# The first unit of an up-projection as eight plain products, with its rows first in the last attention head

## The chip, the cores and the metric

The kernel runs on one core of a Trainium2 chip. The core has a matrix engine (TensorE, called PE; PEld is its loading of weights), a vector engine (VectorE, DVE), an engine for activations and copies (ScalarE, ACT), a general engine (GpSimd, POOL), and a queue that only issues transfers here (SyncE, SP). Each engine works off its own queue in order. Matmul results go to eight PSUM banks; all else lies in SBUF, in buffers that are handed out from pools. The metric is the time of one execution on the device in microseconds (us), as the median of several runs.

## What is computed

One inference step of a one-layer encoder. Rows are 1024 new prompt frames with 16 learned meta rows ahead of them, and 32 frames of a running stream, 1072 rows in all, 1024 wide. Four mixers run side by side (RG-LRU, forgetting attention, stick-breaking attention, gated DeltaNet). Their concatenated, normalised outputs go through `w_o`, are added to the residual and layer-normalised; then comes a convolutional feed-forward part with D_FF = 2816:

```python
x = layer_norm(ALPHA * x + m, P['ln1_g'][l], P['ln1_b'][l])     # m: the mixers through w_o
f, fbuf = conv_ffn(x, st_l['ffn_conv'], P['ffn_w_in'][l], P['ffn_conv_w'][l], P['ffn_conv_b'][l], P['ffn_w_out'][l])
x = layer_norm(ALPHA * x + f, P['ln2_g'][l], P['ln2_b'][l])

def conv_ffn(x, buf, w_in, conv_w, conv_b, w_out):
    gate, up = jnp.split(x @ w_in, 2, axis=-1)
    gate_c, new_buf = causal_dwconv(gate, buf, conv_w, conv_b)
    return (jax.nn.gelu(gate_c) * up) @ w_out, new_buf
```

Everything is fp32. Each large product is made of three matmuls on a high and a low half of both operands: `hi` is a rounded copy (ACT), `lo` the rest (a subtraction), and hi·hi + lo·hi + hi·lo is summed in PSUM.

## The kernel before, in words

The rows lie in nine blocks: block 0 has 48 rows (32 running frames, 16 meta rows), blocks 1 to 8 have 128 each. The program is written as a sequence with priorities, and a planner makes each engine's queue from it: whenever an engine is free in the planner's own account, it takes the instruction with the lowest priority number among those that are ready. A tile from a pool has to wait for a buffer, also where a new pool is laid over the memory of an old one.

*The end of the attention* (`attention`, L1444). Heads run one after the other, the four stick-breaking ones ("s") and then the four forgetting ones ("f"). Each head visits the row blocks in the order `ROWS`, one block in a step (block 8 takes two). Value products are made for the blocks (7, 8), (0, 1, 2), (5, 6) and (3, 4) together. In the last head a finished block goes on at once: `w_o_units("f")` (L1733) multiplies it by the mixer's part of `w_o`, two halves of six matmuls, and DVE adds the scaled result to `h` (L181); two blocks later `ln1_rows` (L1822) takes its statistics on DVE, normalises it on ACT (L144) and stores it as `hn` (SP, L1832). The order of the blocks there is `WROWS`.

*The up-projection* (`ffn_up`, L2017). D_FF is cut into 22 feature tiles of 128; a unit is a pair of them, for the gate (even units) or for the up half (odd units), so there are 22 units. The rows are cut into two parts: part 0 holds blocks 5 to 8 (512 columns, two halves L and R of 256), part 1 blocks 0 to 4 (two halves of 274, which overlap by two). The 1024 inputs are cut in two halves as well, 1 and 2. So an operand is L1, R1, L2 or R2, and a unit times a part is a 2x2 product by blocks. It is made in seven products in place of eight (Strassen in Winograd's form): with sums of operands T1 = R1 - L1, T2 = R2 - T1, T3 = R2 - R1, T4 = L2 - T2 and with four sums of weights (`w_sums`, L1926). Each product (`ffn_product`, L1954) is 12 matmuls (L1959). `STEPS` gives the seven with their PSUM banks a, b, c; `ffn_evac` (L1962) combines the banks: ft is a copy, `fu` is ft plus bank b, after which bank b is added to again by T3, then fv and the outputs.

*Its beginning* (`x_ops`, L1867). For each part, `x_turn` (L1836) transposes the rows on PE and ACT and DVE take them out with gain and bias as `xr` (left half on ACT, L144; right half on DVE, L178). Then the four sums and the seven splits into `xh` and `xl` are made, the sums on DVE except T1, the splits' low halves on DVE for L1, T2, T3, T4 and on POOL for L2, T1, R2. Unit 0 runs part 0 whole and then part 1 whole, its weights split anew for each; from unit 1 on both parts take each step together. `w_load` (L1913) loads a unit's weights in two transfers, `w_split` (L1937) makes a step's halves (ACT, POOL) into four buffers, some steps ahead. `ffn_conv` (L2002) makes convolution and GeLU of a gate tile when its unit ends: four sums on DVE (L181) for each tile, two activations on ACT and the GeLU.

Of the kernel before, what the change touches and what calls it, by code (L numbers as in the profile page):

```python
# [16 lines left out]
P = 128  # L17
# [35 lines left out]
class Gen:  # L53
# [97 lines left out]
    @contextmanager  # L151
    def first(self):

        p = self.tc.cur_priority
        self.tc.cur_priority = p - 100000
        yield
        self.tc.cur_priority = p + (self.tc.cur_priority - (p - 100000))

# [203 lines left out]
    def split_w(self, src, ap, n, m, after=None, gain=None):  # L362
# [13 lines left out]
        return hi, lo  # L376

# [1066 lines left out]
    def attention(self, past):  # L1444

        runs = [(key, h, j, c) for key in "sf" for h in range(4) for j in ROWS for c in reversed(self.attn_chunks(j))]
# [29 lines left out]
        while t < len(runs) + 5 or pairs or late:  # L1476
# [46 lines left out]
            while late and late[0][0] <= t:  # L1523
# [5 lines left out]
                if i > 1:  # L1529
                    self.ln1_rows(WROWS[i - 2])  # L1530
            t += 1
# [335 lines left out]
    def x_ops(self, part, tags, between):  # L1867

        nc = self.nc
        w = NP[part][2]  # L1870
        tags = iter(tags)
        new = lambda: self.U("xr", F32, 4 * w)
        v = lambda t: t.rearrange("p (k m) -> p k m", k=4)
        ops = self.xo[part] = {}

        def split(name, t, eng):
            hi, lo = (self.U(x, F32R, 4 * w, next(tags)) for x in ("xh", "xl"))
            self.act(hi, t, AF.Copy)
            self.tt(lo, t, hi.bitcast(F32), OP.subtract, eng)
            ops[name] = v(hi), v(lo)  # L1880
            between()

        def turn(half):
            l, r = new(), new()
            for k in range(4):
                self.x_turn(part, 4 * half + k, [v(l)[:, k], v(r)[:, k]])
            return l, r

        l1, r1 = turn(0)
        t1 = new()  # L1890
        self.tt(t1, r1, l1, OP.subtract, nc.gpsimd)
        between()
        split("L1", l1, nc.vector)
        l2, r2 = turn(1)
        t2, t3 = l1, r1
        self.tt(t2, r2, t1, OP.subtract)
        split("T2", t2, nc.vector)
        split("L2", l2, nc.gpsimd)
        self.tt(t3, r2, r1, OP.subtract)
        split("T3", t3, nc.vector)  # L1900
        split("T1", t1, nc.gpsimd)
        self.tt(l2, l2, t2, OP.subtract)
        split("T4", l2, nc.vector)
        split("R2", r2, nc.gpsimd)

    def ln1(self):
# [4 lines left out]
        self.xo = {}  # L1911
# [36 lines left out]
    def ffn_steps(self, u):  # L1948

        if u == 0:  # L1950
            return [(n, i) for n in range(2) for i in range(7)]
# [453 lines left out]
```

## Time and profile before

| what | value |
|---|---|
| median of 3 runs | 1634.52 us (1634.32 to 1641.63) |
| profiled execution | 1628.62 us, its span 1626.9 us |
| mean granted TensorE clock | 0.963 |
| busy: PE, PEld, DVE, ACT, POOL | 92%, 82%, 58%, 43%, 55% |
| end of the attention to end of unit 1 | 824 to 917 us |

The profile is of one execution, and times in it count from the start of its span; the median of the runs is 5.9 us over the profiled execution. Busy time of matmuls overlaps, so a busy PE isn't PE at its peak: the number of matmuls in a stretch tells more. A list in order of time gives for each instruction its start, its length, and in brackets the idle time ahead of it with what ended it. A line number can be a helper's (L172 is every two-input operation, L143 and L144 every activation), so operations are told by their tiles.

### The profile page before, as it was taken

How to read it: one execution, taken by the hardware profiler on the slowest of the kernel's cores; microseconds unless marked ns; L12 is line 12 of the kernel's file. 1: busy time of each engine (PE TensorE's matmuls, PEld its weight loads, DVE VectorE, ACT ScalarE, POOL GpSimd, SP SyncE). 2: the span in 40 equal slices, each digit the busy share in tenths (PEclk: the TensorE clock that was granted, in tenths of full speed). 3: DMA queues.
4: the chain of work that ended last, by engine and by line, in shares of the span. 5: the costliest groups of instructions: out<-in, count | busy, mean ns of one | idle time of the engine just before them, and what ended most of it. 6: DMA issues, size and time to landing. Idle time of an engine off the chain costs nothing.

```text
span 1626.9 us, 27257 instructions
## 1 busy us (share of the span) xinstructions
PE 1492.8 (92%) x10200; PEld 1328.3 (82%) x10200; DVE 941.9 (58%) x1802; ACT 697.5 (43%) x1331; POOL 894.9 (55%) x850
## 2 busy tenths in 40 slices
PE   5988998879998898999977999999999999999996
PEld 4878986778777776778756899999999998878774
DVE  9826549863443487678887444444445552355465
ACT  4534624333233455687765233333333354333241
POOL 4473333343234445420159777776676769767575
PEclk9989999999998999999978999999999999999998
DMA  5251121232255645332121222212222256635461
GB/s 162 53 170 52 60 61 40 72 95 63 78 157 148 173 131 148 95 96 68 35 104 52 79 80 79 68 66 79 79 66 67 79 197 230 236 117 194 144 210 38
DMA packets 150092, 171.72 MB, mean 106 GB/s; under 512 B 29546, under 2 KB 126516, under 8 KB 149960
## 3 DMA queue, kind: packets, MB, share of 16 engines
q1 hardware_dynamic: 124025, 140.20, 27.6%
q10 hardware_dynamic: 25839, 29.77, 5.6%
q8 instruction: 81, 1.33, 0.3%
q14 instruction: 51, 0.42, 0.1%
q0 software_dynamic: 96, 0.01, 0.0%
HBM read 123.82 MB, written 46.12 MB: 104 GB/s over the span
## 4 chain that ended last, share of the span: by engine, by line
PE 48%; DVE 10%; POOL 6%; ACT 4%; issue 4%; DMA 3%; ACTq 0%; SPq 0%; DVEq 0%; POOLq 0%
PE ps L184 15%; PE ps L1959 15%; PE mm L184 9%; PE mm L1959 5%; DVE fy L181 3%; PE pw L184 2%; POOL wlo L172 2%; PE ps L188 2%; POOL wl L172 1%; DVE ws L172 1%; DVE sbe L1578 1%; DVE h L181 1%; DMA wr<-in_ffn_w_in 1%; POOL h L172 1%; DVE fx L172 1%
## 5 line engine op out<-in xcount | busy, mean ns | idle before, releaser
L1959 PE MATMUL ps<-xh,whi 128*128 128x256 f32 (+1 forms) x920 | 268.1, 291 | 18.4 <-DVE fu L172 10.4
L1959 PE MATMUL ps<-xl,whi 128*128 128x256 f32 (+1 forms) x920 | 265.9, 289 | 2.2 <-DVE xl L172 1.8
L1959 PE MATMUL ps<-xh,wlo 128*128 128x256 f32 (+1 forms) x920 | 265.4, 288 | 0.0
L1959 PEld LDWEIGHTS ps<-xh,whi 128*128 128x128 f32 x920 | 176.8, 192 | 23.1 <-DVE fu L172 13.0
L1959 PEld LDWEIGHTS ps<-xl,whi 128*128 128x128 f32 x920 | 176.7, 192 | 3.1 <-DVE xl L172 2.3
L1959 PEld LDWEIGHTS ps<-xh,wlo 128*128 128x128 f32 x920 | 176.5, 192 | 0.3
L172 POOL TENSOR_TENSOR wl<-wr,wh 128x1024 fp32r<-128x1024 f32 x58 | 149.6, 2589 | 31.8 <-ACT wh L143 31.7
L172 POOL TENSOR_TENSOR wlo<-ws,whi 128x512 fp32r<-128x512 f32 x92 | 128.0, 1392 | 29.3 <-ACT whi L143 21.9
L172 POOL TENSOR_TENSOR wlo<-wst,whi 128x512 fp32r<-128x512 f32 x56 | 78.7, 1412 | 75.4 <-ACT whi L143 61.8
L143 ACT ACTIVATE wh<-wr 128x1024 fp32r<-128x1024 f32 x58 | 60.8, 1058 | 125.3 <-POOL wl L172 110.0
L172 POOL TENSOR_TENSOR wlo<-wr,whi 128x512 fp32r<-128x512 f32 x69 | 93.7, 1358 | 36.6 <-ACT whi L143 36.6
L172 DVE TENSOR_TENSOR al<-ax,ah 128x768 fp32r<-128x768 f32 (+1 forms) x33 | 60.5, 1833 | 85.8 <-ACT ah L143 72.7
L143 ACT ACTIVATE whi<-ws 128x512 fp32r<-128x512 f32 x92 | 57.8, 628 | 120.0 <-POOL fx L2056 50.1
L184 PE MATMUL ps<-wh,ah 128*128 128x512 f32 x264 | 104.3, 395 | 2.0 <-DVE h L172 2.0
L184 PE MATMUL ps<-wh,al 128*128 128x512 f32 x264 | 104.1, 394 | 0.0
L184 PE MATMUL ps<-wl,ah 128*128 128x512 f32 x264 | 104.0, 394 | 0.0
L181 DVE SCALAR_TENSOR_TENSOR fy<-fx,cf,fy 128x546 f32<-128x546 f32 (+1 forms) x88 | 96.9, 1116 | 12.0 <-ACT fy L144 9.8
L1959 PE MATMUL mm<-xl,whi 128*128 128x274 f32 (+1 forms) x312 | 90.1, 289 | 3.6 <-POOL xl L172 2.9
L1959 PE MATMUL mm<-xh,whi 128*128 128x274 f32 (+1 forms) x312 | 90.1, 289 | 2.0 <-ACT whi L143 0.7
L1959 PE MATMUL mm<-xh,wlo 128*128 128x274 f32 (+1 forms) x312 | 89.6, 287 | 0.0
L184 PE MATMUL mm<-hh,whi 128*128 128x384 f32 (+1 forms) x240 | 87.8, 366 | 1.2 <-ACT ks L1220 1.2
L184 PE MATMUL mm<-hh,wlo 128*128 128x384 f32 (+1 forms) x240 | 82.9, 346 | 1.4 <-POOL wlo L172 1.4
(527 smaller groups left out, 4339.7 us busy)
## 6 DMA issues: line engine op xcount, KB each, us to landing
wr<-in_ffn_w_out SPq DMA_DIRECT2D x58, 512.0 KB
wr<-in_ffn_w_in SPq DMA_DIRECT2D x44, 512.0 KB
actd<-fy ACTq DMA_DIRECT2D x22, 529.0 KB
wst<-in_w_in SPq DMA_DIRECT2D x44, 256.0 KB
ax<-actd SPq DMA_DIRECT2D x22, 384.0 KB
x<-in_x_prompt SPq DMA_DIRECT2D x8, 512.0 KB
hd<-x SPq DMA_DIRECT2D x8, 512.0 KB
qr<-scrs SPq DMA_DIRECT2D x64, 64.0 KB
```

The costliest lines, as they stand in the source:

```text
L143: return self.nc.scalar.activation(out, in_, f, scale=scale, **k)
L172: return (eng or self.nc.vector).tensor_tensor(out, a, b, op)
L181: return (eng or self.nc.vector).scalar_tensor_tensor(out, a, s, b, op0, op1)
L184: return self.nc.tensor.matmul(out, l, r, start=start, stop=stop)
L188: return self.nc.tensor.transpose(out, in_, self.ident[:n, :n])
L1578: self.nc.vector.tensor_tensor_scan(e[:, ::-1], e[:, ::-1], one.to_broadcast([n, w]), one if first else carry, OP.mult, OP.mult)
L1959: self.nc.tensor.matmul(ps, l[:, k], r[:, k], start=start and k + j == 0, stop=stop and k == 3 and j == 2, skip_group_check=not start)
```

## The change

Unit 0 is made in eight plain products for each part, without sums: L1 and R1 with the weights of input half 1, L2 and R2 with those of half 2, each for the two feature tiles; two products share a bank, and ACT copies the banks out. The weights come in four loads of a quarter (512 inputs by 128 features) with one split each, placed ahead of the last row block's products. The operands' sums are made later, beside unit 0 (T1, T3, T2) and in unit 1 (T4); T3, T1 and T4 are split in unit 1. All these run on DVE, and the high halves on ACT. Transposes and splits of part 0 get the priority of the place just ahead of the last block's products. In the last head blocks 6 and 5 come ahead of 1 and 2, and `WROWS` follows it, for all four mixers. Unit 0's convolution and GeLU stand in unit 1, behind its first products.

```diff
+    @contextmanager
+    def at(self, p):
+
+        now, self.tc.cur_priority = self.tc.cur_priority, p
+        yield
+        self.tc.cur_priority = now
...
+    def load_quarter(self, ap):
+
+        return [t.rearrange("p (k m) -> p k m", k=4) for t in self.split_w(None, ap, 4, P)]
...
-        runs = [(key, h, j, c) for key in "sf" for h in range(4) for j in ROWS for c in reversed(self.attn_chunks(j))]
+        runs = [(key, h, j, c) for key in "sf" for h in range(4)
+                for j in (ROWS_F if (key, h) == ("f", 3) else ROWS) for c in reversed(self.attn_chunks(j))]
...
                 if i > 1:
                     self.ln1_rows(WROWS[i - 2])
+                if i == BEFORE:
+                    ld = 2 * DFF
+                    self.w_first = [self.load_quarter(AP(self.I["ffn_w_in"], 512 * half * ld + P * f,
+                                                         [[ld, P], [P * ld, 4], [1, P]])) for half in range(2) for f in range(2)]
+                    self.before_last = self.tc.cur_priority
...
-    def x_ops(self, part, tags, between):
...
+    def x_raw(self, part, half):
+
         w = NP[part][2]
+        for side in "LR":
+            self.xr[part][f"{side}{half + 1}"] = self.U("xr", F32, 4 * w)
+        out = [self.xr[part][f"{side}{half + 1}"].rearrange("p (k m) -> p k m", k=4) for side in "LR"]
+        for k in range(4):
+            self.x_turn(part, 4 * half + k, [o[:, k] for o in out])
+
+    def x_split(self, part, name, tag="T"):
+
+        w = NP[part][2]
+        t = self.xr[part][name]
+        hi, lo = (self.U(x, F32R, 4 * w, tag) for x in ("xh", "xl"))
+        self.act(hi, t, AF.Copy)
+        self.tt(lo, t, hi.bitcast(F32), OP.subtract)
+        self.xo[part][name] = tuple(a.rearrange("p (k m) -> p k m", k=4) for a in (hi, lo))
+
+    def x_sums(self, part, names):
+
+        r = self.xr[part]
+        for name in names:
+            a, b = {"T1": ("R1", "L1"), "T3": ("R2", "R1"), "T2": ("R2", "T1"), "T4": ("L2", "T2")}[name]
+            out = {"T1": "L1", "T3": "R1", "T2": "R2", "T4": "L2"}[name]
+            self.tt(r[out], r[a], r[b], OP.subtract)
+            r[name] = r[out]
+
+    def ffn_first(self, ahead):
+
+        nc = self.nc
+        w = self.w_first
+        banks = {}
+        self.fo[0] = [self.U("fx", F32, UW, "T") for _ in range(2)]
+        for j, xp in enumerate(self.fo[0]):
+            nc.gpsimd.tensor_copy(xp[:, 0:2], self.ffn_state[:, j:44:22])
+
+        def products(part, name):
+            half = int(name[1]) - 1
+            for f in range(2):
+                if not half:
+                    banks[part, f, name[0]] = self.MM()[:, :NP[part][2]]
+                self.ffn_product(banks[part, f, name[0]], w[2 * half + f], self.xo[part][name], not half, True)
+                if half:
+                    c0 = 2 + NP[part]["LR".index(name[0])]
+                    self.act(self.fo[0][f][:, c0:c0 + NP[part][2]], banks[part, f, name[0]], AF.Copy)
+
+        with self.at(self.before_last):
+            self.x_raw(0, 0)
+            self.x_split(0, "L1")
+            self.x_split(0, "R1")
+            self.x_raw(0, 1)
+            self.x_split(0, "L2")
+            self.x_split(0, "R2")
+        products(0, "L1")
+        products(0, "R1")
+        products(0, "L2")
+        self.x_raw(1, 0)
+        self.w_load(1)
+        products(0, "R2")
+        self.x_raw(1, 1)
+        self.x_split(1, "L1")
+        self.x_split(1, "R1")
+        products(1, "L1")
+        self.x_split(1, "L2")
+        products(1, "R1")
+        self.x_split(1, "R2")
+        products(1, "L2")
+        self.x_sums(0, ("T1", "T3", "T2"))
+        self.x_split(0, "T2", "U")
+        ahead(2)
+        products(1, "R2")
+        self.x_sums(1, ("T1", "T3", "T2"))
+        self.x_split(1, "T2", "U")
+
+    def x_late(self, name):
+
+        if name == "T4":
+            for part in range(2):
+                self.x_sums(part, ("T4",))
+        for part in range(2):
+            self.x_split(part, name, "T" if name == "T4" and not part else "U")
...
-        self.w_load(0)
-        self.w_sums(0)
-        self.x_ops(0, ["T"] * 7 + ["U"] * 7, lambda: ahead(min(nxt + 1, 4)))
+        self.ffn_first(ahead)
         for u, p, i in order:
...
             ahead(todo.index(key) + 4)
+            if u == 1 and p == 0 and i < 2:
+                for name in (("T3", "T1"), ("T4",))[i]:
+                    self.x_late(name)
             self.ffn_product(st[p][bank], split[key], self.xo[p][self.STEPS[i][0]], start, True)
             self.ffn_evac(u, p, i, st[p])
...
+            if u == 1 and p and i == 0:
+                self.ffn_conv(0, 1)
+                self.ffn_conv(0, 0)
...
 ROWS = [0, 8, 7, 1, 2, 6, 5, 3, 4]
-WROWS = [7, 8, 0, 1, 2, 5, 6, 3, 4]
+ROWS_F = [0, 8, 7, 6, 5, 1, 2, 3, 4]
+WROWS = [7, 8, 5, 6, 0, 1, 2, 3, 4]
+BEFORE = 8
```

Left out: the new attributes set in `ln1`, the special order and keys of unit 0 that fall away in `ffn_steps` and `ffn_up`, and the condition under which the convolution's result tiles are taken.

## Rows read from the trace of the kernel before

**Rows 1.** Busy time of the span by engine, from the page (TensorE).

```profile
PE 1492.8 (92%) x10200; PEld 1328.3 (82%) x10200; DVE 941.9 (58%) x1802; ACT 697.5 (43%) x1331; POOL 894.9 (55%) x850
```

**Rows 2.** Stretches: start:end, length, busy us (instructions) by engine, PE clock, DMA share, GB/s.

```profile
805.00:830.00 25.00, 20.58 (x106) 16.45 (x105) 23.24 (x93) 15.50 (x37) 5.79 (x9) 0.97 0.47 172
835.00:850.00 15.00, 10.49 (x42) 8.54 (x41) 10.18 (x9) 8.91 (x15) 15.00 (x9) 0.53 0.00 0
850.00:873.00 23.00, 15.61 (x109) 13.15 (x108) 16.77 (x28) 14.28 (x22) 20.99 (x14) 1.00 0.01 1
873.00:887.00 14.00, 10.04 (x43) 9.42 (x44) 10.80 (x8) 6.32 (x8) 12.77 (x6) 0.63 0.42 123
907.20:917.60 10.40, 10.40 (x86) 10.40 (x86) 3.31 (x8) 1.90 (x3) 8.23 (x9) 1.00 0.17 50
```

**Rows 3.** PE in order of time: start, length, what; in brackets idle before.

```profile
824.19 0.39 PE L184 MATMUL mm<-lwl,chi 128*128 128x512 f32 x1
835.86 0.58 PE L1959 MATMUL ps<-xh,whi 128*128 128x256 f32 x1 [0.21 <-ACT xh L143]
...
904.20 0.58 PE L1959 MATMUL ps<-xh,whi 128*128 128x256 f32 x1 [3.80 <-DVE fu L172]
...
917.46 0.29 PE L1959 MATMUL ps<-xh,whi 128*128 128x256 f32 x1
```

**Rows 4.** What PE waited for, 824 to 925 us: total us, times, longest.

```profile
PE ps L1959 <- DVE fu L172: 6.9, 2, 3.8
PE ps L1959 <- ACT xh L143: 5.9, 3, 2.9
```

**Rows 5.** DVE, then POOL, in order of time: large subtractions, some side by side.

```profile
839.58 4.49 DVE L172 TENSOR_TENSOR xr<-xr,xr 128x1024 f32<-128x1024 f32 x2 [0.47 <-POOL xr L172]
843.99 2.30 DVE L172 TENSOR_TENSOR xl<-xr,xh 128x1024 fp32r<-128x1024 f32 x1
850.93 1.22 DVE L172 TENSOR_TENSOR xl<-xr,xh 128x1024 fp32r<-128x1024 f32 x1
872.95 1.29 DVE L172 TENSOR_TENSOR xl<-xr,xh 128x1096 fp32r<-128x1096 f32 x1
...
834.94 1.27 POOL L172 TENSOR_TENSOR wlo<-wr,whi 128x512 fp32r<-128x512 f32 x1 [2.16 <-ACT whi L143]
842.94 4.48 POOL L172 TENSOR_TENSOR wlo<-ws,whi 128x512 fp32r<-128x512 f32 x2
```

**Rows 6.** Matmuls on the weight buffers, by tile, 700 to 840; POOL's first sum.

```profile
L184 PE MATMUL mm<-whi,chi x32: 387/396/483, 706.1 to 771.8; 128*128 128x512 f32 x28, 128*48 128x512 f32 x4
...
828.63 1.27 POOL L172 TENSOR_TENSOR ws<-wr 128x512 f32<-128x512 f32 x1 [10.26 <-DMA wr<-in_ffn_w_in]
```

**Rows 7.** DVE groups by shape, 824 to 920 us: busy us, mean ns, idle.

```profile
L178 DVE TENSOR_SCALAR xr<-ps,cf 128x256 f32<-128x256 f32 x16 | 8.1, 535 | 1.9 <-ACT xr L144 1.6 <-PE ps L188 0.3
L178 DVE TENSOR_SCALAR xr<-ps,cf 128x18 f32<-128x18 f32 x8 | 2.3, 289 | 0.1
```

**Rows 8.** By tile, whole run: count, ns min/median/max, first and last start.

```profile
L181 DVE SCALAR_TENSOR_TENSOR fy<-fx,cf,fy x88: 751/789/1820, 891.9 to 1325.9; 128x546 f32<-128x546 f32 x44, 128x512 f32<-128x512 f32 x44
...
L172 DVE TENSOR_TENSOR ws<-wr,wr x22: 678/694/1954, 830.0 to 1296.1; 128x512 f32<-128x512 f32 x22
```

**Rows 9.** In order of time: unit 0's convolution, unit 1's fu (DVE); POOL.

```profile
891.92 11.89 DVE L181 SCALAR_TENSOR_TENSOR fy<-fx,cf,fy 128x546 f32<-128x546 f32 x8 [0.43 <-ACT fy L144]
...
903.74 0.76 DVE L172 TENSOR_TENSOR fu<-ft,ps 128x256 f32<-128x256 f32 x2
...
898.11 3.45 POOL L172 TENSOR_TENSOR wlo<-ws,whi 128x512 fp32r<-128x512 f32 x2
```

**Rows 10.** SP's waits, 800 to 900 us; normalisations on ACT, by tile.

```profile
SPq L1922 <- PE mm L184: 0.2, 1, 0.2
...
L144 ACT ACTIVATE h<-h,bmv x9: 1227/1244/1247, 803.3 to 831.2; 128x1024 f32<-128x1024 f32 x8, 48x1024 f32<-48x1024 f32 x1
```

More of the change, by code (lines that the diff above doesn't have):

```diff
@@ L1865, in x_turn @@
             at += n
-    def x_ops(self, part, tags, between):
-        nc = self.nc
[L1870 to L1904, printed above, removed]
@@ new lines, in x_raw @@
+    def x_raw(self, part, half):
[6 more added lines that the diff above has]
+    def x_split(self, part, name, tag="T"):
+        w = NP[part][2]
+        t = self.xr[part][name]
[3 more added lines that the diff above has]
+        self.xo[part][name] = tuple(a.rearrange("p (k m) -> p k m", k=4) for a in (hi, lo))
@@ L1910, in ln1 @@
         nc.vector.tensor_copy(self.sel[:, NS:34], self.ident[:48, 46:48])
-        self.xo = {}
+        self.xo, self.xr = [{}, {}], [{}, {}]
     def w_load(self, u):
@@ L1948, in ffn_steps @@
     def ffn_steps(self, u):
-        if u == 0:
-            return [(n, i) for n in range(2) for i in range(7)]
         return [(n, i) for i in range(7) for n in range(2)]
@@ L2019, in ffn_up @@
         units = 2 * (NFT // 2)
-        order = [(u, p, i) for u in range(units) for p, i in self.ffn_steps(u)]
-        todo = []
-        for u, p, i in order:
-            key = (u, p if u == 0 else 0, i)
-            if key not in todo:
-                todo.append(key)
+        order = [(u, p, i) for u in range(1, units) for p, i in self.ffn_steps(u)]
+        todo = [(u, i) for u in range(1, units) for i in range(7)]
         self.actd = self.dp.tile([NFT, P, FT], F32, name="actd", tag="actd")
@@ L2033, in ahead @@
             while nxt < min(upto, len(todo)):
-                u, p, i = todo[nxt]
+                u, i = todo[nxt]
                 if u not in sums:
                     sums.add(u)
-                    if u:
-                        self.w_sums(u)
-                    if u and u + 1 < units:
+                    self.w_sums(u)
+                    if u + 1 < units:
                         self.w_load(u + 1)
@@ L2042, in ahead @@
                 nxt += 1
-        self.w_load(0)
-        self.w_sums(0)
-        self.x_ops(0, ["T"] * 7 + ["U"] * 7, lambda: ahead(min(nxt + 1, 4)))
+        self.ffn_first(ahead)
         for u, p, i in order:
             up = u % 2
-            if (u, p, i) == (0, 1, 0):
-                self.x_ops(1, ["U"] * 7 + ["T"] * 7, lambda: None)
-                self.w_load(1)
-            key = (u, p if u == 0 else 0, i)
+            key = (u, i)
             if not up and i == 0 and p == 0:
@@ L2067, in ffn_up @@
             last = (p, i) == self.ffn_steps(u)[-1]
-            if not up and i == 0 and p == 0:
+            if i == 0 and p == 0 and (u == 1 or not up):
                 self.fo[1] = [self.U("fy", F32, FT) for _ in range(2)]
+            if u == 1 and p and i == 0:
+                self.ffn_conv(0, 1)
+                self.ffn_conv(0, 0)
             if not up and p and i >= 5:
```

## The prediction

> **What bounds the kernel now.** TensorE (PE) is busy for 92% of the span [rows 1], so an edit pays where PE is kept waiting or runs slow. I read the table by stretches first, then what PE waited for, then the lists in order of time of the engines that it waited for. In the table [rows 2] the reader is to see a hole. From 907.2 us on, 86 matmuls take 10.4 us at full clock, 0.121 us each, and PE has no gap. Between 830 and 907.2 us PE is never that dense for long: 42 matmuls in 15 us from 835, 109 in 23 us from 850, 43 in 14 us from 873, with a mean granted clock of 0.53 in the first and 0.63 in the third of these stretches: most of their time passes at the lower of its two levels (1.2 of 2.4 GHz).
>
> The end marks are in [rows 3]. The last matmul of the attention tail starts at 824.19, the first product of the up-projection at 835.86, and the second unit ends at 917.46, where the third starts. That is 93 us for 72 transposes, 168 matmuls of unit 0 and 168 of unit 1. At 0.121 us for all, with the transposes a little slower, it is about 50 us of work. Some 43 us are lost, and this is the most that the change can touch: everything behind it (units 2 to 21, the down-projection) stays as it is.
>
> Who makes PE wait? The list of waits [rows 4] names DVE's fu (the sum that frees a PSUM bank) for 6.9 us and ACT's xh for 5.9. Both are ends of a longer queue. GpSimd (POOL) is busy for 15.00 of 15 us, 20.99 of 23 and 12.77 of 14 in the same stretches [rows 2]: it makes low halves of weights and of operands, and DVE works beside it at a price. A DVE subtraction of 1024 columns took 1.22 us with POOL idle on two-input work, and 2.30 us beside two POOL subtractions that took 4.48 us together, where one took 1.27 us alone [rows 5].
>
> **The change part by part.** *Products.* Seven products for each part become eight: 16 x 12 = 192 matmuls instead of 168, +24 x 0.121 = **+2.9 us** of PE.
>
> *Weights of unit 0.* Out go 14 splits of weights (7 for each part) and four sums of weights; in come four splits, from four loads of a quarter each (the same bytes as the two loads of before). They are put on SP behind the hn stores of rows done by then. The four hi/lo buffers are free, as the stick-breaking mixer last used them at 772 us [rows 6], and ACT and POOL have room in the tail (15.50 and 5.79 of 25 us). I cost them at nothing. If the cover were gone, the price is that of before: POOL had the first load 10.26 us after its earlier work, at 828.6 [rows 6], about 4 us behind the tail's last matmul.
>
> *Operands: POOL to DVE.* All sums and splits of operands now run on DVE. POOL loses 2 sums, 6 splits, 10 weight splits and 2 weight sums. DVE goes from 8 splits to 16 and from 6 sums to 8, and loses the 10 small fu/fv/fx sums of unit 0 and two weight sums. So POOL, the bound of 835 to 887, is freed, and **DVE becomes the engine to count**.
>
> *Rows and order.* Rows 5 to 8 go first, so part 0's operands can be made beside the last rows. But DVE is busy for 23.24 of the 25 us from 805 to 830 [rows 2]: what is put there pushes the rest back. I therefore count DVE as full from 805 on, its tail ending at 830 as now, and add what must come before the fu of unit 1, in DVE's queue. The new last-head order leaves five rows instead of four for the end (a row costs DVE two sums and two statistics), while the attention steps there get shorter; I take it as even, +-3 us.
>
> DVE's queue after 830, uncontended: part 0's right halves 8 x 0.53 = 4.3 us, and part 1's 8 x 0.53 + 8 x 0.29 = 6.6 [rows 7]; eight splits of L1, R1, L2, R2, 4 x 1.22 + 4 x 1.29 = 10.1 [rows 5]; sums T1, T3, T2 of both parts, 3 x 1.22 + 3 x 1.29 = 7.5; two T2 splits 2.5; the weight sums of unit 1, 2 x 0.69 = 1.4 [rows 8]. This is 32.4 us, so T2 is ready near 862 plus what contention adds. Then what the change moves into unit 1: T3 and T1 splits 5.0, the convolution of unit 0, 8 x 0.77 = 6.2 [rows 8], T4's sums and splits 5.0, two fu 0.9. Together **49.5 us**.
>
> To it come contention and idle time. About ten POOL subtractions and sums of 1.3 us remain beside it (seven weight splits of unit 1, its two sums, one or two of unit 2), 13 us. The rows give 1.08 us lost for 1.27 us of POOL beside a subtraction, 0.85 for one [rows 5]; beside the convolution its eight pieces took 11.89 us in place of 8 x 0.77 = 6.2 [rows 8, 9], 5.7 lost beside six such pieces of POOL (the last two in 3.45 us) [rows 9], about 0.75 for 1 us of POOL's own work. I take 0.75, **10 us**, with 0 and 31 as ends (no overlap; every large operation at the contended price). For idle moments, where part 1's evacuations wait behind PE's products, I take 2.5 us. So fu is done at 830 + 49.5 + 10 + 2.5 = **892**.
>
> PE in between: from 824.4, 32 transposes (4.3 us), 2 us until L1 is split, eight products (11.6), 40 transposes (5), eight products (11.9) end near 860; L1, T2 and L2 of unit 1 follow, held a few us for T2's split. Then T3 adds to the bank that fu reads and waits for it. This wait is already in the trace: unit 1's fu stood behind the pieces of the convolution until 903.74, and PE waited 3.80 us for it [rows 3, 9]. In the new queue T3, T1, the convolution and T4 all stand ahead of fu. So I expect PE to sit from about 870 to 892, one long wait in place of many short ones. The eight products left take what they took before, 904.2 to 917.46 = 13.3 us [rows 3], the half-clock start included: **unit 1 ends at 905.3 instead of 917.5, a gain of 12.2 us**.
>
> One rule speaks against the change. In the trace both sides slow down together: 2.30 us of DVE stand beside 2.24 of POOL for work of 1.22 and 1.27 us [rows 5]. The Trainium skill, "SBUF — State Buffer", section "Who interferes with whom", says that a DVE instruction with two SBUF inputs and a GpSimd one that reads SBUF hold the shared pair for the whole instruction, so the other fully blocks. By it the 13 us of POOL would be added whole, and the gain would be 9 us; the rows of the convolution show less than that.
>
> **The rivals.** *PE-bound* (A): the queue order that the planner makes puts fu ahead of T4 or of the convolution, since the planner takes whatever is ready. Then T3 and T1 run while DVE makes T4; only T4's split at about 891 binds, with four products (5.9 us) behind it: 897, gain 20. If part of the operands is really made in gaps of the tail, up to 30. For it: DVE is idle 1.76 us in the tail and PE 4.4. Against it: in before, PE twice waited for an fu that was queued behind larger work [rows 4].
>
> *Contention eats it* (B): POOL's work costs DVE one for one and the fifth late row its 4 us: 892 becomes 895 to 900, gain 4 to 9, about 1628. For it: POOL's subtractions beside DVE's in [rows 5] come near it. Against: POOL has lost over half of its work here.
>
> *Slower* (C): one mechanism, DVE at the contended price throughout. 16 splits lose 1.08 us each, 8 sums 1.03 (two took 4.49 us) [rows 5], 8 convolution pieces 0.72 (eight took 11.89 us) [rows 9]: 17.3 + 8.2 + 5.7 = 31.2 us where I took 10. Then fu comes at 913.2 and unit 1 ends at 926.5, 9 us later than now: 1643.5. It turns to a loss from 22 us of contention on, which needs POOL busy through three quarters of the stretch; by the list above it keeps some 15 of 60.
>
> *The move does nothing* (D): the first buffers of the new pool lie on the weights of the last w_o rows. The first load of before waited for a matmul there [rows 10], and the last row was normalised from 831.2 on. If part 0's operand buffers do so too, the early start is void and part 0 begins at 824 as now. In my count that costs little, since DVE is full either way: gain 8 to 13, inside the forecast.
>
> **How the numbers follow.** The profiled execution took 1628.62 us (span 1626.9), the median of the runs is 1634.52; I take the gain from the median: 1634.52 - 12.2 = **1622.3**, in the profiled execution 1616.4. A measurement of this kernel can tell about 0.5%, 8.2 us, from no change. Chances: forecast with D (gain 8 to 18, of which a little lies under 8.2) 0.45; A (18 to 30) 0.23; B and all that moves it less than 8.2 us either way 0.25; C 0.07. So faster 0.67, same 0.26, slower 0.07. The range leaves out C, the far end of A and the weak end of B: 1607 to 1633.
>
> **What would show it.** Right: POOL well under half busy from 835 to 890; DVE over 90% from 805 to about 890; first product near 830; a wait of PE for DVE's fu of 10 to 20 us before T3 of unit 1; unit 1's last product near 905. Wrong: fu early in DVE's queue with T4's split as the last wait (A); subtractions of 2 us and more on DVE (B, C); a gap of PE or DVE before 824 that was not there (the tail). If the time changes outside 780 to 920 us, my place is wrong.

## The result, and the profile of the changed kernel

| | before | changed |
|---|---|---|
| median | 1636.43 us (1634.32 to 1641.63) | 1613.91 us (1607.25 to 1616.75) |
| ratio to before, 95% interval | | 0.9852 [0.9812, 0.9892] |
| profiled execution (its span) | 1628.62 (1626.9) us | 1614.18 (1612.4) us |
| mean granted clock | 0.963 | 0.969 |

The kernel became 22.5 us faster; forecast were 12.2 us and a median of 1622.3, with a range of 1607 to 1633. The direction and the place were right; the size is that of rival A (20 us). The page shows 24 matmuls more, as costed, and POOL with 39 us less of work [rows 1]:

```profile
PE 1490.2 (92%) x10224; PEld 1326.1 (82%) x10224; DVE 946.0 (59%) x1800; ACT 693.4 (43%) x1327; POOL 856.1 (53%) x830
```

Before the two traces can be laid side by side, one thing has to be taken out. Up to the first products with `w_o` the code is the same (from there on the order of the rows differs), yet these start at 547.6 us before and at 552.9 after, and the first matmul of the last mixer's `w_o` products (tile lwh) at 789.0 and 794.2. The table by stretches shows why. Columns: stretch, length, busy us (instructions) of PE, PEld, DVE, ACT, POOL, PE clock, DMA share, GB/s. From 100 to 200 us, first before and then after:

```profile
100.00:200.00 100.00, 95.32 (x620) 94.33 (x618) 46.93 (x79) 48.72 (x87) 37.94 (x54) 0.94 0.30 91
...
100.00:200.00 100.00, 95.33 (x592) 94.33 (x592) 44.24 (x77) 45.09 (x82) 37.31 (x53) 0.89 0.29 89
```

PE is equally busy, but the granted clock was 0.94 in the one execution and 0.89 in the other, and 28 matmuls fewer were done. That has nothing to do with the change: the profile of conv_late (below), the changed kernel with one line moved in unit 1, has 0.97 there. So all marks below count from that first matmul, and a time of the changed kernel less 5.2 us can be held against one of before. By these marks the up-projection ends 19.4 us earlier (552.4 and 533.0 us), and what follows it is the same (285.5 and 285.2): the gain lies in the stretch that the forecast named.

The same stretches as in [rows 2], 5 us later, of the changed kernel:

```profile
810.00:835.00 25.00, 21.00 (x108) 15.72 (x108) 22.83 (x90) 15.27 (x36) 4.58 (x9) 1.00 0.32 126
835.00:840.00 5.00, 4.71 (x20) 4.41 (x21) 4.93 (x14) 4.97 (x9) 0.00 (x0) 0.51 0.07 26
840.00:855.00 15.00, 15.00 (x113) 13.99 (x112) 10.81 (x21) 9.69 (x15) 1.78 (x2) 0.94 0.64 211
855.00:878.00 23.00, 20.52 (x152) 19.69 (x151) 19.25 (x21) 13.89 (x22) 15.45 (x8) 0.96 0.00 1
878.00:892.00 14.00, 11.20 (x84) 10.76 (x82) 14.00 (x14) 8.31 (x11) 9.16 (x5) 0.95 0.12 39
...
810.20:895.30 85.10, 74.96 (x484) 67.14 (x484) 74.91 (x154) 53.03 (x90) 32.98 (x23) 0.93 0.23 81
835.20:895.30 60.10, 54.16 (x376) 51.59 (x377) 52.09 (x66) 37.76 (x56) 28.60 (x15) 0.90 0.19 63
```

The third line is to be read against the second of [rows 2]: 113 matmuls in 15 us where 42 were, at clock 0.94 and not 0.53, with POOL at 1.78 us and not at 15.00. In the fifth line DVE has no idle moment: 14.00 of 14. The last two are 805 to 890 and 830 to 890 by the times of before, for the sums further down.

PE in order of time (start, length, instruction; in brackets idle before it and what ended it), to be held against [rows 3]:

```profile
829.97 0.48 PE L191 MATMUL mm<-lwl,chi 128*128 128x512 f32 x1
...
835.29 0.79 PE L2017 MATMUL ps<-xh,whi 128*128 128x256 f32 x2 [2.14 <-ACT xh L143]
...
869.17 0.29 PE L2017 MATMUL ps<-xh,wlo 128*128 128x274 f32 x1
...
875.38 0.38 PE L2017 MATMUL mm<-xh,wlo 128*128 128x256 f32 x1 [1.81 <-POOL wlo L179]
...
882.66 0.28 PE L2017 MATMUL mm<-xh,whi 128*128 128x256 f32 x1
...
891.09 0.39 PE L2017 MATMUL ps<-xh,whi 128*128 128x256 f32 x1 [2.39 <-ACT whi L143]
...
896.43 0.42 PE L2017 MATMUL mm<-xh,whi 128*128 128x256 f32 x1 [0.65 <-DVE fv L179]
...
902.32 0.42 PE L2017 MATMUL ps<-xh,wlo 128*128 128x274 f32 x2
```

These are the end of the tail, the first product, the end of unit 0, a matmul of unit 1's T2 that waits for POOL, T3, a product of unit 2 (its L1, drawn ahead of T4), T4, and the end of unit 1, at 897.1 by the times of before. T3, for which a wait of 10 to 20 us was forecast, has none. What PE waited for from 820 to 915 us (us, times, longest; three entries below 1.2 us left out), against [rows 4]:

```profile
PE ps L2017 <- ACT whi L143: 2.4, 1, 2.4
PE ps L2017 <- ACT xh L143: 2.1, 1, 2.1
PE mm L2017 <- POOL wlo L179: 1.8, 1, 1.8
PE ps L2017 <- POOL wlo L179: 1.6, 2, 1.0
PE ps L2017 <- ACT ft L143: 1.2, 1, 1.2
```

There is no entry for fu. DVE in order of time shows why, to be held against [rows 5, 9]:

```profile
874.60 4.12 DVE L179 TENSOR_TENSOR xl<-xr,xh 128x1096 fp32r<-128x1096 f32 x2 [3.14 <-ACT xh L143]
878.64 0.41 DVE L179 TENSOR_TENSOR fu<-ft,mm 128x256 f32<-128x256 f32 x1
878.97 4.28 DVE L179 TENSOR_TENSOR xl<-xr,xh 128x1096 fp32r<-128x1096 f32 x2
883.17 0.43 DVE L179 TENSOR_TENSOR fu<-ft,mm 128x274 f32<-128x274 f32 x1
883.52 2.04 DVE L179 TENSOR_TENSOR xl<-xr,xh 128x1096 fp32r<-128x1096 f32 x1
885.48 7.58 DVE L188 SCALAR_TENSOR_TENSOR fy<-fx,cf,fy 128x546 f32<-128x546 f32 x8
892.99 2.38 DVE L179 TENSOR_TENSOR xl<-xr,xh 128x1096 fp32r<-128x1096 f32 x1
```

Both fu stand between the splits, ahead of the convolution and of T4's last split: the planner did not keep the order of the program, and this is the order of rival A.

### The profile page after: what moved, and what is told of

The parts are those of the page before. It is cut to its first block, busy times and chain, and to the rows that moved or that the text cites. A ratio compares the mean times of both kernels' runs of the same rounds, so it can differ in the third digit from the quotient of the medians.

```text
span 1612.4 us, 27248 instructions
## 1 busy us (share of the span) xinstructions
PE 1490.2 (92%) x10224; PEld 1326.1 (82%) x10224; DVE 946.0 (59%) x1800; ACT 693.4 (43%) x1327; POOL 856.1 (53%) x830
## 4 chain that ended last, share of the span: by engine, by line
PE 40%; DVE 11%; POOL 9%; ACT 6%; issue 6%; DMA 4%; SPq 0%; ACTq 0%; DVEq 0%; POOLq 0%
PE ps L191 12%; PE ps L2017 12%; PE mm L191 8%; PE mm L2017 4%; DVE fy L188 3%; POOL wl L179 3%; POOL wlo L179 3%; PE ps L195 2%; DMA wr<-in_ffn_w_in 2%; PE pw L191 2%; POOL h L179 1%; DVE sbe L1595 1%; DVE h L179 1%; ACT s L144 1%; ACT fy L144 1%
## 5 line engine op out<-in xcount | busy, mean ns | idle before, releaser
L179 POOL TENSOR_TENSOR wlo<-wst,whi 128x512 fp32r<-128x512 f32 x60 | 82.9, 1387 | 100.1 <-ACT whi L143 70.4
L179 POOL TENSOR_TENSOR wlo<-ws,whi 128x512 fp32r<-128x512 f32 x84 | 115.3, 1374 | 28.5 <-ACT whi L143 20.3
L191 PE MATMUL ps<-wh,ah 128*128 128x512 f32 x308 | 121.5, 395 | 3.6 <-DVE h L179 3.6
L191 PE MATMUL ps<-wh,al 128*128 128x512 f32 x308 | 121.7, 395 | 2.3 <-DVE al L179 2.3
L191 PE MATMUL ps<-wl,ah 128*128 128x512 f32 x308 | 121.4, 394 | 0.0
L143 ACT ACTIVATE wh<-wr 128x1024 fp32r<-128x1024 f32 x58 | 60.7, 1057 | 120.3 <-POOL wl L179 107.8
L179 DVE TENSOR_TENSOR al<-ax,ah 128x768 fp32r<-128x768 f32 (+1 forms) x33 | 65.1, 1975 | 77.2 <-ACT ah L143 66.3
L143 ACT ACTIVATE whi<-ws 128x512 fp32r<-128x512 f32 x84 | 52.5, 626 | 116.2 <-POOL fx L2104 57.7
L2017 PE MATMUL mm<-xh,whi 128*128 128x256 f32 (+1 forms) x320 | 92.5, 289 | 2.4 <-DVE fu L179 1.8
L2017 PE MATMUL mm<-xh,wlo 128*128 128x256 f32 (+1 forms) x320 | 92.0, 287 | 1.8 <-POOL wlo L179 1.8
L2017 PE MATMUL mm<-xl,whi 128*128 128x256 f32 (+1 forms) x320 | 91.8, 287 | 0.0
```

What stands on the lines that cost most here:

```text
L143: return self.nc.scalar.activation(out, in_, f, scale=scale, **k)
L179: return (eng or self.nc.vector).tensor_tensor(out, a, b, op)
L191: return self.nc.tensor.matmul(out, l, r, start=start, stop=stop)
L2017: self.nc.tensor.matmul(ps, l[:, k], r[:, k], start=start and k + j == 0, stop=stop and k == 3 and j == 2, skip_group_check=not start)
```

## The experiments

By the intervals of the table a measurement of the whole kernel is good to 3 to 7 us, and several edits are worth less. So each run gives its ratio to the kernel before and, from the list of PE in order of time, marks in us from the first matmul on lwh: the start of the first product, and the starts of the last matmul of unit 0, of unit 1 and of the whole up-projection. (The end of unit 1 is found by counting 168 matmuls past unit 0, so a product of unit 2 that is drawn ahead counts too: the last matmul of the changed kernel's own unit 1 starts at 108.1, its mark is 106.0.) Where an expectation speaks of the stretch, that is the last mark. The changed kernel stands there twice; between its two profiles the last two marks differ by 2.6 us, so under 3 us isn't told apart.

| run | ratio to before, 95% | median us | first product | unit 0 ends | unit 1 ends | up-projection ends |
|---|---|---|---|---|---|---|
| before | | 1632.9 to 1636.4 | 46.9 | 101.6 | 128.3 | 552.4 |
| changed | 0.9852 [0.9812, 0.9892] | 1613.91 | 41.1 | 75.0 | 106.0 | 533.0 |
| again | 0.9873 [0.9851, 0.9895] | 1613.98 | 41.1 | 72.4 | 103.4 | 530.4 |
| rows_old | 0.9878 [0.9855, 0.9902] | 1614.59 | 44.2 | 77.7 | 110.8 | 535.4 |
| no_early | 0.9874 [0.9855, 0.9892] | 1614.86 | 40.7 | 74.2 | 107.1 | 533.0 |
| fu_last | 0.9871 [0.9848, 0.9894] | 1613.98 | 41.1 | 73.7 | 109.2 | 535.3 |
| pool_back | 0.9920 [0.9891, 0.9950] | 1619.66 | 41.7 | 80.1 | 114.0 | 541.7 |
| t1_pool | 0.9878 [0.9847, 0.9909] | 1613.80 | 41.7 | 74.5 | 107.8 | 533.3 |
| conv_late | 0.9852 [0.9820, 0.9884] | 1607.28 | 41.1 | 73.6 | 105.6 | 531.5 |
| w_late | 0.9890 [0.9859, 0.9922] | 1616.60 | 43.3 | 76.1 | 107.1 | 534.1 |
| before_dve | 0.9978 [0.9950, 1.0006] | 1628.25 | 46.8 | 99.6 | 123.8 | 551.1 |
| plain_only | 0.9945 [0.9922, 0.9968] | 1621.16 | 45.9 | 81.4 | 116.6 | 541.1 |
| w1_dve | 0.9888 [0.9857, 0.9919] | 1612.50 | 43.3 | 76.1 | 107.8 | 536.2 |
| w1_dve_conv | 0.9882 [0.9838, 0.9925] | 1608.93 | 41.1 | 72.4 | 103.4 | 529.6 |

**The changed kernel again**, as it is.

> The changed kernel once more, as the mark for the runs beside it. Both theories: a ratio of 0.981 to 0.989 to before, and the stretch from the first w_o matmul of the last mixer to the last product of the up-projection at 533 us +-1.5 (552.4 in before), as the identical code ahead of it differs by some us from run to run.

It confirms the gain with an interval half as wide. Its stretch, 530.4 us, lies below the 533 +-1.5 that were expected. The granted clock tells why; this is to be held against the changed kernel's 835 to 840 us, also from its first product on:

```profile
838.80:843.80 5.00, 4.61 (x34) 4.20 (x35) 4.93 (x14) 4.97 (x9) 0.00 (x0) 1.00 0.08 32
```

At clock 1.00 PE made 34 matmuls in these 5 us, at 0.51 only 20. Of the matmuls of units 0 and 1, 77 started at the lower clock in before, 53 in the changed kernel and 13 here. One follows the other after 0.21 us at the lower level (1.2 GHz; at 838.14 and 838.35 us in the changed kernel) and 0.12 us at the upper (2.4 GHz; at 840.98 and 841.10 us here), which makes some 7, 5 and 1 us. So, by this estimate, 2 to 6 of the 19 to 22 us of gain are a PE that ran at the upper clock for longer; no run holds the clock fixed.

**The row order alone undone** (rows_old).

```diff
-ROWS_F = [0, 8, 7, 6, 5, 1, 2, 3, 4]
-WROWS = [7, 8, 5, 6, 0, 1, 2, 3, 4]
+ROWS_F = ROWS
+WROWS = [7, 8, 0, 1, 2, 5, 6, 3, 4]
```

> The changed kernel with the old order of the rows (last head and w_o). Theory 1 (POOL freed and DVE full: what counts is the sum of DVE's queue): the stretch is 0 to 4 us longer than that of the changed kernel. Theory 2 (the early start of part 0's operands, which needs rows 5 to 8 first, is where the gain is): 6 to 12 us longer.

The first product comes 3.1 us later, and unit 1 ends 4.8 us later than in the changed kernel, 7.4 later than in its second profile. The ratio doesn't show it. At the end of the up-projection it is 2.4 and 5.0 us, so the order is worth a few us, nearer to theory 1 than to theory 2.

**The early place alone undone** (no_early): part 0's preparation stays where it stands in the program.

```diff
-        with self.at(self.before_last):
+        if True:
```

> The changed kernel, with part 0's transposes and splits at their ordinary place behind the last row instead of ahead of it. Theory 1 (DVE's sum counts): 0 to 3 us longer than the changed kernel. Theory 2 (early start): 5 to 10 us longer, first product that much later against the end of the tail.

Nothing: first product at 40.7, the up-projection's end the same as in the changed kernel. With the rows ordered so, the planner draws part 0's work ahead by itself.

**fu behind T4's splits** (fu_last): the place that the forecast gave it, forced by an order between the last split of the operands and unit 1's two fu.

```diff
+            r = self.tt(st["u2"], st["t"], b, OP.add)
+            if self.lo_last is not None and self.fu_wait:
+                self.order(r.ins, self.lo_last)
```

> The changed kernel with unit 1's two fu held behind T4's last split in DVE's queue, the place that the prediction gave them. If the place of fu is the step that failed: PE waits for fu before T3 of unit 1 for 10 us or more, and the stretch is 5 to 9 us longer, near the 12 us of gain that were forecast. If T4's last split binds anyway: under 2 us longer.

DVE in this run:

```profile
884.98 5.52 DVE L188 SCALAR_TENSOR_TENSOR fy<-fx,cf,fy 128x546 f32<-128x546 f32 x8
890.42 1.29 DVE L179 TENSOR_TENSOR xl<-xr,xh 128x1096 fp32r<-128x1096 f32 x1
891.63 0.76 DVE L179 TENSOR_TENSOR fu<-ft,mm 128x256 f32<-128x256 f32 x2
```

and two of PE's starts (idle before them in brackets):

```profile
890.05 0.58 PE L2017 MATMUL ps<-xh,whi 128*128 128x256 f32 x1 [3.28 <-ACT whi L143]
...
894.11 0.58 PE L2017 MATMUL ps<-xh,wlo 128*128 128x256 f32 x1 [2.81 <-POOL wlo L179]
```

The first lwh matmul of this profile is at 795.0, so fu ends 97.4 us after it; the forecast (892 against 789.0) had 103. DVE got there 5.6 us sooner: its eight convolution pieces took 5.52 us, 0.69 each, as POOL had nothing to do from 883.9 to 889.6 us. And no wait for fu appears: the planner put other products, L1 of unit 2 among them, ahead of T3, and PE's two longest waits are for the weights of those. Unit 1 ends 3.2 us later than in the changed kernel (5.8 by its second profile), and the up-projection 2.3 (4.9), not 8. Neither expectation came as a whole: the wait is not there, and the loss lies between the two. So the place of fu is a part of what the forecast missed; the rest is that neither queue is fixed, DVE's nor PE's: where one thing would wait, another is put in.

**Operands back to POOL** (pool_back): the splits of L2, T1 and R2 and the sum T1 where they were.

```diff
-        self.tt(lo, t, hi.bitcast(F32), OP.subtract)
+        self.tt(lo, t, hi.bitcast(F32), OP.subtract, self.nc.gpsimd if name in POOLED else None)
...
-            self.tt(r[out], r[a], r[b], OP.subtract)
+            self.tt(r[out], r[a], r[b], OP.subtract, self.nc.gpsimd if name == "T1" else None)
...
+POOLED = "L2", "T1", "R2"
```

> The changed kernel with the low halves of L2, T1 and R2 and the sum T1 back on POOL, where before had them. Theory 1 (the gain is the work taken from POOL): the stretch 5 to 15 us longer than the changed kernel, POOL over 80% busy between first product and unit 2. Theory 2 (the gain is that products can start without sums): under 2 us longer.

Unit 1 ends 8.0 us later (10.6 by the second profile), as theory 1 had it, though POOL was busy for 76% between first product and unit 2 and not for over 80%. What PE waited for, and the convolution on DVE:

```profile
PE ps L2017 <- POOL wlo L179: 4.5, 2, 4.2
PE ps L2017 <- POOL xl L179: 4.2, 3, 2.0
PE mm L2017 <- DVE fu L179: 3.7, 1, 3.7
...
877.15 12.65 DVE L188 SCALAR_TENSOR_TENSOR fy<-fx,cf,fy 128x546 f32<-128x546 f32 x8
...
892.00 0.43 DVE L179 TENSOR_TENSOR fu<-ft,mm 128x274 f32<-128x274 f32 x1
```

The move takes work off POOL, and it also makes DVE's own faster: the same eight pieces took 12.65 us here, 7.58 in the changed kernel. Part 1's fu falls behind the convolution again, as in the kernel before, and PE waits 3.7 us for it.

**T1's low halves alone on POOL** (t1_pool).

```diff
+POOLED = "T1",
```

> The changed kernel with only the two T1 splits on POOL. If DVE's queue up to T4's last split sets the end: T4's last split comes 2 to 4 us earlier and the stretch is 0 to 3 us shorter. If the two engines block each other: T1's low half comes late, PE waits for POOL, 2 to 6 us longer.

The stretch is the same within the spread (533.3). T4's split does not come earlier: it ends 101.8 us after the first lwh matmul, where the changed kernel has 101.2, for the eight convolution pieces took 11.1 us beside the busier POOL in place of 7.58, and PE waited 3.2 us for POOL's xl. So less work on DVE's list did not shorten its queue. Whether the loss in the run before comes from the amount of work or from L2, R2 and the sum T1, which stood back there too, wasn't separated.

**The convolution one step later** (conv_late).

```diff
-            if u == 1 and p and i == 0:
+            if u == 1 and p and i == 1:
```

> The changed kernel with unit 0's convolution queued behind T4 instead of ahead of it. If T4's last split, behind eight convolution pieces on DVE, is what ends unit 1: the split comes 6 to 8 us earlier and the stretch is 2 to 5 us shorter. If the gate's GeLU is needed as soon: PE waits for the sums that read it, 0 to 4 us longer.

DVE in this run, whose first lwh matmul is at 788.2 us:

```profile
876.20 4.34 DVE L179 TENSOR_TENSOR xl<-xr,xh 128x1096 fp32r<-128x1096 f32 x2
880.47 1.79 DVE L188 SCALAR_TENSOR_TENSOR fy<-fx,cf,fy 128x546 f32<-128x546 f32 x1
...
882.51 4.85 DVE L188 SCALAR_TENSOR_TENSOR fy<-fx,cf,fy 128x546 f32<-128x546 f32 x6
887.29 0.43 DVE L179 TENSOR_TENSOR fv<-ft,mm 128x274 f32<-128x274 f32 x1
```

and what PE waited for longest:

```profile
PE mm L2017 <- DVE fv L179: 5.1, 2, 3.5
```

The operands' last split ends 92.3 us after it, where in the changed kernel it ends at 101.2; unit 1 ends as in the changed kernel (105.6), since now fv stands behind the convolution, and PE waits for that. So the place of T4's split by itself does not set the end. It fits a bound by the sum of DVE's work up to the end of unit 1, but doesn't show one: two splits fewer on DVE (t1_pool) and nine operations more (w1_dve, below) both end unit 1 at 107.8. The median is the lowest of all; the interval of the ratio lies within the changed kernel's.

**The quarter loads later** (w_late): placed where part 0's preparation is written.

> The changed kernel with the four quarter loads and their splits issued at the start of unit 0 instead of ahead of the last row. If the weights were covered (as costed, nothing): under 1 us longer, since the first product waits for its operand until then anyway. If the early place of the loads is part of the gain: 3 to 5 us longer, with PE waiting for wlo or whi at the first product.

The tail took 38.0 us in this profile, up to the last matmul on lwh, in place of 35.5; the first product comes 2.2 us later and unit 1 ends 1.1 us later (3.7 by the second profile). PE's wait at the first product is for xh, 2.04 us, not for weights. The profile of w1_dve, with the loads in their early place, has the same 38.0. So the price of nothing that the forecast set on the loads holds within the spread.

**Before, with the operands on DVE** (before_dve).

```diff
-            self.tt(lo, t, hi.bitcast(F32), OP.subtract, eng)
+            self.tt(lo, t, hi.bitcast(F32), OP.subtract)
...
-        self.tt(t1, r1, l1, OP.subtract, nc.gpsimd)
+        self.tt(t1, r1, l1, OP.subtract)
```

> The kernel before with one thing changed: every operand sum and low half of the up-projection's beginning runs on DVE (POOL loses 6 splits and 2 sums), while the Strassen products, the 14 weight splits of unit 0 and the row order stay. Theory 1 (POOL was the bound of 835 to 887, so freeing it is worth something by itself): unit 0 ends 3 to 10 us earlier, counted from the tail's first matmul (the kernel before: 101.6 us), and the time is 3 to 10 us below the kernel before. Theory 2 (the relief needs the plain products, since POOL still has 14 weight splits and 4 weight sums ahead of them): within 2 us of the kernel before.

Unit 0 ends 2.0 us earlier, unit 1 4.5. The interval reaches from 8 us faster to 1 us slower, so by the time it is open whether theory 1 or 2 holds; by the marks it is 2: the whole up-projection ends only 1.3 us earlier. Taking the operands off POOL is a small part by itself. That POOL also has 10 weight splits and 2 weight sums less in the changed kernel isn't tested here.

**Plain products alone** (plain_only): the changed kernel with the edits of rows_old, no_early and pool_back together, so that only the eight products, their four quarter loads and the late sums stay.

> The changed kernel with the row order, the place of part 0's preparation and POOL's share of the operands (splits of L2, T1 and R2, the sum T1) as in the kernel before: of the change there remain the plain products of unit 0, its four quarter loads with four splits, and the late sums. Theory 1 (the plain products carry the part that no other edit accounts for): about 10 us below the kernel before, the mark after unit 1 near 116 to 120 us (before 128.3, changed 106.0). Theory 2 (relief of POOL is all there is, and it needs both): 0 to 3 us below the kernel before, the mark near 126 to 128.

Unit 1 ends at 116.6, as theory 1 had it, and the time is 0.55% [0.32, 0.78] below before.

**Unit 1's weights on DVE** (w1_dve): two weight sums and seven low halves of weights.

```diff
-        self.tt(s3, a11, a21, OP.subtract, nc.gpsimd)
-        self.tt(s4, a12, s2, OP.subtract, nc.gpsimd)
+        self.tt(s3, a11, a21, OP.subtract, None if u == 1 else nc.gpsimd)
+        self.tt(s4, a12, s2, OP.subtract, None if u == 1 else nc.gpsimd)
...
-        self.tt(lo, src, hi.bitcast(F32), OP.subtract, nc.gpsimd)
+        self.tt(lo, src, hi.bitcast(F32), OP.subtract, None if u == 1 else nc.gpsimd)
```

> The changed kernel with unit 1's last two weight sums and its seven low halves on DVE instead of POOL (nine operations of 0.69 us). Theory 1 (what is left of the loss is POOL blocked beside DVE: its 1.27 us become up to 7.76 us, and PE waits for them): 2 to 6 us shorter than the changed kernel, and no wait of PE for POOL's wlo before unit 2. Theory 2 (DVE is full from 845 to 895, so each operation that is put there is added whole): 9 x 0.69 = 6.2 us longer, less what POOL's absence gives back, so 0 to 6 us longer.

The waits for POOL are gone, and another has come. DVE, then PE:

```profile
872.70 7.57 DVE L188 SCALAR_TENSOR_TENSOR fy<-fx,cf,fy 128x546 f32<-128x546 f32 x8
880.19 1.28 DVE L179 TENSOR_TENSOR xl<-xr,xh 128x1096 fp32r<-128x1096 f32 x1
881.40 0.76 DVE L179 TENSOR_TENSOR fu<-ft,mm 128x256 f32<-128x256 f32 x2
...
881.86 0.58 PE L2017 MATMUL mm<-xh,whi 128*128 128x256 f32 x1 [5.89 <-DVE fu L179]
```

Here the planner did put the convolution and T4's split ahead of fu, and PE has the one long wait for fu that the forecast described, 5.89 us. The nine operations bring at most what they cost (unit 1 ends 1.8 us later, the up-projection 3.2); theory 1 falls for the gain.

**The same with the convolution one step later** (w1_dve_conv: both edits).

> The kernel of the run before this, with unit 0's convolution and GeLU placed one step later in unit 1. If both edits help by themselves they add: 3 to 7 us shorter than the changed kernel. If DVE is full and the order of its work decides nothing more: as the run before, within 2 us.

Unit 1 ends at 103.4, the mark of the second profile of the changed kernel, and 4.4 us ahead of the run before it, where the second theory had 2 at most; by the ratios the two differ by 1 us. Neither this nor conv_late can be told from the changed kernel, so no better version was found.

**Where the gain comes from**, by the marks (us, from the table):

| | first product | unit 0 takes | unit 1 takes | unit 1 ends |
|---|---|---|---|---|
| before | 46.9 | 54.7 | 26.7 | 128.3 |
| before_dve | 46.8 | 52.8 | 24.2 | 123.8 |
| plain_only | 45.9 | 35.5 | 35.2 | 116.6 |
| pool_back | 41.7 | 38.4 | 33.9 | 114.0 |
| changed | 41.1 | 33.9 | 31.0 | 106.0 |

The plain products, which come with four weight splits in place of 14 and with late sums, shorten unit 0 by 19.2 us (54.7 to 35.5). Whether the missing sums or the 10 missing splits on POOL count for more wasn't separated. They give 8.5 back in unit 1, which now makes sums and splits beside its own products. The row order starts the first product 4.2 us earlier (plain_only to pool_back, with the early place, which had no effect when it alone was undone), but with the operands on POOL nothing of it is left at the end of the up-projection (541.1 and 541.7). The operands' move from POOL to DVE takes another 8.0 us off (pool_back to changed; 8.7 at the end of the up-projection), against 4.5 in the kernel before (1.3): it is worth more beside the plain products. So at the end of the up-projection the plain products make 11.3 us of the 19.4, the operands' move, with the row order, the rest. The clock's share (above) is in these numbers.

## Why the prediction was right in direction and too small

*Products.* 24 matmuls more: 10224 in place of 10200. Right.

*Tail and rows.* "I take it as even, +-3 us": the tail's last matmul is at 829.97, less 5.2 is 824.8, against 824.19. Right. The first product was forecast near 830 and came at 835.29 - 5.2 = 830.1.

*Weights of unit 0 at nothing.* Right within the spread (w_late).

*POOL.* Forecast well under half busy from 835 to 890. It is busy for 28.60 of the 60.1 us from 835.2 to 895.3, 48%: under half, but not well under; one of its operations alone took 7.76 us (last section).

*DVE's sum.* Forecast 49.5 us of work, 10 of contention and 2.5 idle, so that T4's split ends near 891. It ends at 892.99 + 2.38 = 895.37, or 890.2 by the times of before. Its parts came out otherwise. From 835.2 to 895.3 DVE is busy for 52.09 us (87%; over 805 to 890, for which over 90% was forecast, 88%) where 59.5 were forecast, and idle for 8.0, not 2.5; 3.14 of these stand at 874.60, where it waits for ACT's high half. Contention was smaller: the five groups shown without fu took 20.4 us, where six splits of 1.22 to 1.29 [rows 5] and eight pieces of 0.77 [rows 8] make 13.7; with 1.0 us at 867.87 (last section) that is some 8 us, not 10. Some 2.6 us of the sum, five of part 0's right halves, had run ahead of 835.2, in the tail. So the end is right because less work and more idle time, 7.4 and 5.5 us, nearly cancelled: in part that is luck.

*A row read wrongly.* The 1.22 us "with POOL idle on two-input work" [rows 5] were not that. In the trace of before a POOL subtraction starts 0.09 us behind that DVE one and stands beside it:

```profile
851.02 2.28 POOL L172 TENSOR_TENSOR wlo<-wr,whi 128x512 fp32r<-128x512 f32 x1
```

DVE kept its own pace there, and POOL took 2.28 us for 1.27. So the price of 0.75 to 0.85 us of DVE for each us of POOL holds where POOL's operation had begun first; where DVE's had, these rows show POOL paying. The forecast charged that price for every POOL operation.

*The Trainium skill's rule.* "SBUF — State Buffer", section "Who interferes with whom", had the other engine fully blocked, and the gain at 9 us. The trace agrees with the blocking: one POOL subtraction took 7.76 us beside DVE's two-input work, where 1.27 is its own time (below). It does not agree with the sum: part of the blocking fell on POOL, as in these two cases, and DVE lost some 8 us, not 13.

*Where it failed: fu's place.* "In the new queue T3, T1, the convolution and T4 all stand ahead of fu" was taken from the order of the program. The planner takes whatever is ready, and both fu went ahead of convolution and T4. So "one long wait in place of many short ones" did not come, T3 and T1 ran from 882.66 on, and behind T4's split stand four products only: unit 1 ends at 902.3 - 5.2 = 897.1 where the forecast had 905.3 and rival A 897. These 8 us are the whole miss in the stretch. A's time was right, but that T4's split alone binds isn't shown: T4's first product waited for fv, which DVE had behind that split (896.43), and by conv_late an earlier split alone brings nothing.

*The error behind it.* With fu forced to its forecast place (fu_last), the loss is 2 to 6 us, not 8, so fu's place is part of the miss and not all of it: the forecast froze PE's queue too, while the planner fills a wait with another ready product (unit 2's L1, at 891.09 in the changed kernel). On the other side w1_dve shows that the forecast's mechanism exists: 5.89 us of PE waiting for an fu behind the convolution. And conv_late puts T4's split 9 us earlier without any gain. The step that held is the end of DVE's work, partly by luck; the steps that failed are those which told the order in it, and the order of PE's.

*Rivals.* B and C: subtractions of about 2 us on DVE are there (4.12 for two, 2.38 for one), but only in the late part where POOL runs beside them; at 858.35 four of this kind took 4.85 us together (last section). C needed POOL busy through three quarters; it was 48%. D: the early place is worth nothing, as D said, though not for D's reason: the early start was there with the program's own order as well. Whether buffers lying on the weights of `w_o` held anything was not tried.

*Median and profile.* The profiled executions differ by 14.5 us of span: 19.4 in the up-projection and 0.3 behind it, less the 5.2 us ahead of the change. The medians differ by 22.5, and by 19 in the second measurement; the 3 us between them are less than what one execution differs from the next ahead of the change.

## What to carry to other kernels

Where a planner makes the queues, a forecast must not line up an engine's work in the order of the program: sum the work that the fullest engine must have done by the end of the stretch (here DVE's, whose end was forecast within 1 us, partly by errors that cancelled), and add only what must stand behind the last of it. That this sum was the bound isn't shown. Plain products ahead, with the sums made beside them, pay when the first operands are what PE waits for: here 19 us in the first unit for 2.9 us of added matmuls, nearly half of it given back in the next. Work that is moved from one engine to another changes the pace of both; so it is worth more or less with each other edit, and is measured in their presence.

## What the runs showed of the hardware

A POOL subtraction of 512 columns, 1.27 us by itself, took 7.76 us. DVE and POOL of the changed kernel in that time:

```profile
858.35 4.85 DVE L179 TENSOR_TENSOR xl<-xr,xh 128x1096 fp32r<-128x1096 f32 x4
863.11 0.69 DVE L179 TENSOR_TENSOR ws<-wr,wr 128x512 f32<-128x512 f32 x1
863.71 1.29 DVE L179 TENSOR_TENSOR xr<-xr,xr 128x1096 f32<-128x1096 f32 x1
...
866.74 1.22 DVE L179 TENSOR_TENSOR xl<-xr,xh 128x1024 fp32r<-128x1024 f32 x1
867.87 3.59 DVE L179 TENSOR_TENSOR xr<-xr,xr 128x1096 f32<-128x1096 f32 x2
...
862.55 7.76 POOL L179 TENSOR_TENSOR wlo<-wr,whi 128x512 fp32r<-128x512 f32 x1 [7.80 <-ACT whi L143]
870.26 2.35 POOL L179 TENSOR_TENSOR ws<-wr 128x512 f32<-128x512 f32 x1
```

A row of DVE operations with two inputs in SBUF ran at its own pace (0.69, 1.22 and 1.29 us) until 869.2, and POOL's one instruction stood; only then did DVE lose about 1 us (3.59 for two of 1.29). So the price is not always shared evenly, as the forecast's 0.75 per us of POOL assumed: a dense run on DVE can hold POOL off. It need not. From 876.4 to 885.6 us DVE is as dense, with one small sum between its splits at 878.64 and one at 883.17, and there the two took turns: DVE's splits took 2.04 to 2.31 us, and POOL's subtractions came through at about twice their own time:

```profile
877.60 4.57 POOL L179 TENSOR_TENSOR wlo<-ws,whi 128x512 fp32r<-128x512 f32 x2
```

What decides between the two isn't shown. Six of the profiles have the long one at 7.75 to 7.76 us and rows_old at 9.45; no_early hasn't (2.01), and its unit 1 ends no earlier: it cost PE little here.

The other is the clock in stages that the change doesn't touch: 5.3 us between two profiles at the same point of the same code (547.6 and 552.9 us), as large as most single edits of this study. Without marks counted from a common instruction the edits of the table could not have been told apart.
